# Softmax cross-entropy gradient: the stores of odd rows issued on GpSimd's queue

## The chip, the cores and the metric

The kernel runs on one NeuronCore of a Trainium2 chip. A core has TensorE (PE), VectorE (DVE), ScalarE (ACT), GpSimd (POOL) and SyncE (SP), which run their own instruction queues and meet only at semaphores. Transfers between HBM (the device's main memory) and SBUF (the core's working memory, 128 partitions) are done by 16 DMA engines; an instruction on an engine's queue issues a transfer, and a semaphore tells when it has landed. The metric is the device time of one execution in microseconds (us), the median of several runs; lower is better.

## The reference

For 8 x 1024 = 8192 rows of 8192 logits (fp32, 268 MB) and a label for each row, the kernel computes the gradient of the cross-entropy loss with respect to the logits: softmax of the row, less 1 at the label's column.

```python
logits_max = np.max(logits, axis=-1, keepdims=True)
exp_logits = np.exp(logits - logits_max)
softmax = exp_logits / np.sum(exp_logits, axis=-1, keepdims=True)
...
one_hot[batch_idx, seq_idx, labels] = 1.0
return (softmax - one_hot).astype(np.float32)
```

Every logit is read once and every result, as large as the input, is written once.

## The kernel before

The 8192 rows are cut into B = 32 blocks. A block has G = 2 rows for each of the 128 partitions: partition p of block b holds the two neighbouring rows `(b p j)` with j = 0 and 1. In this text "row t" (t = 0 to 63) means the 128 rows, one for each partition, with b = t // 2 and j = t % 2: a tile of 128 x 8192 fp32, 4.19 MB, with 32 KB contiguous in a partition. Rows with j = 0 are called even, those with j = 1 odd.

The tile X in SBUF has SLOTS = 3 slots of one block each; block b lies in slot b % 3, and all work on it is done in place: the load writes it, the engines turn it into the result, and the store reads it.

Work on row t:

- DVE: the negated maximum along the row into m (`row_max`, TENSOR_REDUCE).
- ACT: exp(x - max) in place, with the sum into s (first ACTIVATE and its ACTIVATION_READ_ACCUMULATOR).
- DVE: r = 1 / s (RECIPROCAL).
- ACT: x * r in place (second ACTIVATE, out<-in X<-X,r).
- DVE: subtract 1 where the column number equals the label (SCALAR_TENSOR_TENSOR with the column numbers `iota`, which stand in PSUM as 16-bit integers). Its entry in `finished[t]` is what the store of the row waits for.

The last row does the last two steps in two halves of 4096 columns.

The order on each queue is written out by hand by the loop over t. DVE's is: reciprocal of t, maximum of t + 1, subtraction of t. ACT's is: exp of t, store of t - 1, scaling of t. So the maximum of the next row stands ahead of the subtraction of this one, and the store of a row stands in ACT's queue ahead of the scaling of the next.

SP issues the loads, all in order and as far ahead as the waits allow. `LOADS` has a letter for each block: "r" is one transfer per row (two a block, each waits for the store of the same row of the block three before), "w" is one transfer for the whole block (8.39 MB, 64 KB contiguous in a partition; it waits for both stores of that earlier block). Blocks 0 to 4 and 26 to 31 are "r", blocks 5 to 25 are "w". Row 1 of block 2 also waits until `iota` is made, as its place is used for that at the start. `STORES` is "r" for all blocks: one store a row, issued by ACT. At the end ACT waits for the stores of the last three blocks.

Every instruction is recorded by the helper `run`, which adds the waits and the semaphore to count up; the last wait rides on the instruction itself, those before it stand in the engine's queue. So nearly all instructions have one line in the profile, L68 (L69 in the changed kernel), and groups are told apart by engine, operation and tile. Each slot has semaphores `got` (loads, one for each of its two pieces) and `put` (stores, the same). POOL makes an identity matrix and the column numbers in the first 8 us and has nothing to do after that. PE does two small transposes of the labels at the start.

Of the kernel before, what the change touches and what calls it, by code (L numbers as in the profile page):

```python
# [8 lines left out]
G = 2  # L9
SLOTS = 3  # L10
# [7 lines left out]
def kernel(  # L18
# [6 lines left out]
    nc = tc.nc  # L25
# [30 lines left out]
    with tc.tile_critical():  # L56
        sem = tc.alloc_semaphore
        got = [[sem(f"got{i}{q}") for q in range(2)] for i in range(SLOTS)]
        put = [[sem(f"put{i}{q}") for q in range(2)] for i in range(SLOTS)]
        lab_got, dve, act, pe, pool = (sem(n) for n in ("lab_got", "dve", "act", "pe", "pool"))  # L60
        count = {}

        def run(engine, waits, counter, method, **operands):

            waits = list(dict.fromkeys(waits))
            for w in waits[:-1]:
                engine.wait_ge(*w)
            instruction = getattr(engine, method)(**operands)  # L68
            for w in waits[-1:]:  # L69
                instruction._wait_ge(*w)  # L70
            step = 16 if method == "dma_start" else 1
            instruction.then_inc(counter, step)
            count[counter.name] = count.get(counter.name, 0) + step
            return counter, count[counter.name]
# [42 lines left out]
        loaded, stored, finished = {}, {}, []  # L117
# [14 lines left out]
        def store(t):  # L132
            b, j = divmod(t, G)
            stored.setdefault(b, [])
            for q, piece in enumerate(PIECES[STORES[b]]):
                ps, js = piece
                if js.stop != j + 1:
                    continue
                w = run(
                    nc.scalar, [finished[t]], put[b % SLOTS][q], "dma_start",  # L140
                    out=o_b[b, ps, js, :], in_=X[ps, b % SLOTS, js, :],
                )
                stored[b].append((piece, w))
# [16 lines left out]
        for t in range(T):  # L160
# [11 lines left out]
            if t > 0:  # L172
                store(t - 1)
# [10 lines left out]
            for c, w in zip(cols, scaled):  # L184
# [4 lines left out]
                )  # L189
            finished.append(w)  # L190
        store(T - 1)
        for b in range(B - SLOTS, B):
            for _, w in stored[b]:
# [31 lines left out]
```

## Time and profile before

| | |
|---|---|
| median of 3 timed runs | 1247.98 us (1247.91 to 1248.11) |
| span of the profiled execution | 1245.7 us; the profile gives no other time for it |
| DVE busy | 1119.2 us (90%), 196 instructions |
| ACT busy | 919.1 us (74%), 194 instructions |
| POOL busy | 7.4 us (1%), 7 instructions |
| bytes moved | 536.98 MB, mean 431 GB/s over the span |
| maximum of a row (DVE) | 64 x 8675 ns |
| subtraction at the label (DVE) | 65 instructions, a full row 8742 ns |
| exp of a row (ACT) | 64 x 7123 ns |
| scaling of a row (ACT) | 65 instructions, a full row 7122 ns |
| issue of a store on ACT's queue | 64 x 338 ns |
| store, issue to landing | 14.3 us at least, 30.8 median, 52.4 at most |
| load, issue to landing | 12.2 us at least; median 26.6 of one row or 33.4 of a block |

A span runs from the first to the last instruction of the profiled execution. Engines DVE, ACT and POOL are busy while they compute; a DMA issue isn't counted as busy. The 40 digits of a "DMA" line are the busy share of the 16 DMA engines in 40 equal slices of the span, in tenths (9 is 90% or more). The rows "q1", "q10" are DMA queues: packets, megabytes and the time that their packets took as a share of the 16 engines' span; q1 belongs to SP's loads and q10 to ACT's transfers. A packet is one contiguous stretch that a DMA engine moves for one queue, 32 or 64 KB here, or the 4 bytes that count up a semaphore. The chain that ended last is followed back from the last instruction, at each step to what released it.

### The profile page before, as it was taken

How to read it: one execution, taken by the hardware profiler on the slowest of the kernel's cores; microseconds unless marked ns; L12 is line 12 of the kernel's file. 1: busy time of each engine (PE TensorE's matmuls, PEld its weight loads, DVE VectorE, ACT ScalarE, POOL GpSimd, SP SyncE). 2: the span in 40 equal slices, each digit the busy share in tenths (PEclk: the TensorE clock that was granted, in tenths of full speed). 3: DMA queues.
4: the chain of work that ended last, by engine and by line, in shares of the span. 5: the costliest groups of instructions: out<-in, count | busy, mean ns of one | idle time of the engine just before them, and what ended most of it. 6: DMA issues, size and time to landing. Idle time of an engine off the chain costs nothing.

```text
span 1245.7 us, 592 instructions
## 1 busy us (share of the span) xinstructions
PE 0.4 (0%) x2; PEld 0.3 (0%) x2; DVE 1119.2 (90%) x196; ACT 919.1 (74%) x194; POOL 7.4 (1%) x7
## 2 busy tenths in 40 slices
PE   0000000000000000000000000000000000000000
PEld 0000000000000000000000000000000000000000
DVE  5999998888988889888998888988889999999893
ACT  3888886778776787767877778777777788887772
POOL 2000000000000000000000000000000000000000
DMA  9999999999999999999999999999999999999998
GB/s 406 417 429 433 438 433 442 437 426 427 430 435 445 439 417 442 426 430 437 432 443 438 420 435 432 430 437 450 420 426 437 436 428 432 437 435 429 432 437 386
DMA packets 15460, 536.98 MB, mean 431 GB/s; under 512 B 1728, under 2 KB 1728, under 8 KB 1760
## 3 DMA queue, kind: packets, MB, share of 16 engines
q1 hardware_dynamic: 6192, 268.44, 50.0%
q10 hardware_dynamic: 9264, 268.51, 49.9%
q14 instruction: 4, 0.03, 0.0%
HBM read 268.50 MB, written 268.44 MB: 431 GB/s over the span
## 4 chain that ended last, share of the span: by engine, by line
DMA 59%; DVE 37%; another core or an unknown queue 2%; ACT 1%; DVEq 0%; issue 0%; PE 0%; SPq 0%; ACTq 0%
DMA X<-in_logits_dram 31%; DMA out_dram<-X 27%; DVE m L68 18%; DVE X L68 18%; ACT X L68 1%; DVE iota L68 0%; DVEq L56 0%; DMA lab_raw<-in_labels_dram 0%; DVE lab_f L68 0%; DVE r L68 0%; PE iota L68 0%; SPq L68 0%; ACTq L68 0%; DVE lab L68 0%
## 5 line engine op out<-in xcount | busy, mean ns | idle before, releaser
L68 DVE TENSOR_REDUCE m<-X 128x1 f32<-128x8192 f32 x64 | 555.2, 8675 | 94.3 <-DMA X<-in_logits_dram 94.3
L68 ACT ACTIVATE X<-X,m 128x8192 f32<-128x8192 f32 x64 | 455.9, 7123 | 188.4 <-DVE m L68 188.4
L68 DVE SCALAR_TENSOR_TENSOR X<-iota,lab,X 128x8192 f32<-128x8192 int16 (+1 forms) x65 | 559.7, 8612 | 4.1 <-ACT X L68 4.1
L68 ACT ACTIVATE X<-X,r 128x8192 f32<-128x8192 f32 (+1 forms) x65 | 456.0, 7017 | 115.9 <-DVE r L68 115.9
L68 DVE RECIPROCAL r<-s 128x1 f32<-128x1 f32 x64 | 9.9, 154 | 7.3 <-ACT X L68 7.3
L68 ACT ACTIVATION_READ_ACCUMULATOR X<-X,m 128x1 f32 x64 | 12.0, 187 | 0.0
L68 DVE CAST lab_f<-lab_raw 32x256 f32<-32x256 int32 x1 | 3.7, 3685 | 4.7 <-DMA lab_raw<-in_labels_dram 4.7
L68 POOL IOTA X<- 128x8192 int16 x1 | 6.9, 6944 | 0.0
L68 DVE TENSOR_SCALAR iota<-X 128x4096 int32<-128x4096 int32 x1 | 4.4, 4427 | 0.1
L68 ACT ACT_TABLE_LOAD x1 | 1.3, 1283 | 1.3 <-SPq L56 1.3
L68 DVE COPY lab<-iota 128x64 f32<-128x64 f32 x1 | 0.2, 225 | 0.5 <-PE iota L68 0.5
L68 PE MATMUL iota<-ident,lab_f 32*128 32x32 f32 x2 | 0.4, 300 | 8.5 <-DVE lab_f L68 8.5
L68 PEld LDWEIGHTS iota<-ident,lab_f 32*128 32x128 f32 x2 | 0.3, 196 | 8.4 <-DVE lab_f L68 8.4
L68 POOL TENSOR_SCALAR_AFFINE_SELECT ident<-ident 32x32 f32<-32x32 f32 x1 | 0.2, 204 | 0.1
L68 POOL MEMSET ident<- 32x32 f32 x1 | 0.1, 115 | 0.5 <-SPq L56 0.5
L209 POOL MEMSET const-bfloat16-1.0<- 128x1 bf16 x1 | 0.1, 107 | 0.0
L209 POOL MEMSET const-uint8-127<- 128x1 uint8 x1 | 0.1, 107 | 0.0
L209 POOL MEMSET const-float32-0.0<- 128x1 f32 x1 | 0.1, 104 | 0.2 <-issue 0.2
L209 POOL MEMSET const-float32-1.0<- 128x1 f32 x1 | 0.1, 104 | 0.0
## 6 DMA issues: line engine op xcount, KB each, us to landing
out_dram<-X ACTq DMA_DIRECT2D x64, 4096.0 KB, 30.8
X<-in_logits_dram SPq DMA_DIRECT2D x22, 4096.0 KB, 26.6
X<-in_logits_dram SPq DMA_DIRECT2D x21, 33.4
lab_raw<-in_labels_dram ACTq DMA_DIRECT2D x1, 64.0 KB, 3.8
```

Of the source, the lines that this page charges most:

```text
L68: instruction = getattr(engine, method)(**operands)
L209: nc = _bacc.Bacc("TRN2", target_bir_lowering=False, num_devices=1)
```

## The change

The store of an odd row (j = 1) is issued by POOL on POOL's own DMA queue, with a semaphore of its own for each slot (`put_pool`). The store of an even row is issued by ACT as before. Both wait for the same subtraction on DVE (`finished[t]`). The loads, their order and what frees them are unchanged: a load waits for the same stores, whose counters for odd rows are now `put_pool`. The final waits on ACT cover both kinds.

```diff
         got = [[sem(f"got{i}{q}") for q in range(2)] for i in range(SLOTS)]
+        put_pool = [sem(f"put_pool{i}") for i in range(SLOTS)]
         put = [[sem(f"put{i}{q}") for q in range(2)] for i in range(SLOTS)]
...
                 if js.stop != j + 1:
                     continue
+                odd = j == G - 1
                 w = run(
-                    nc.scalar, [finished[t]], put[b % SLOTS][q], "dma_start",
+                    nc.gpsimd if odd else nc.scalar, [finished[t]],
+                    put_pool[b % SLOTS] if odd else put[b % SLOTS][q], "dma_start",
                     out=o_b[b, ps, js, :], in_=X[ps, b % SLOTS, js, :],
                 )
```

In the built program ACT's queue loses 32 transfers, POOL's gets 32, one after the other behind its start-up work, each with a wait for DVE. The instructions of DVE, PE and SP stand in the same order as before.

## The prediction

> **What bounds the kernel now.** I read the slices of the page and its DMA queues first, then the queues' shares in single stretches, then the chain that ended last, then ACT's timeline at the end. The page's DMA line and queue rows:
>
> ```profile
> DMA  9999999999999999999999999999999999999998
> ...
> q1 hardware_dynamic: 6192, 268.44, 50.0%
> q10 hardware_dynamic: 9264, 268.51, 49.9%
> ```
>
> q1 carries the loads (SP), q10 the stores (ACT). Together their packets fill 99.9% of the 16 DMA engines' span: the transfers are the bound, and DVE (90%) waits for them. In the trace's packet records every 32 KB packet took 1213 ns, load or store alike, and each engine moves 8 per row of 4.19 MB, so one row's transfer costs 8 x 1.213 = 9.70 us. 64 loads and 64 stores are 128 x 9.70 = 1242 us of a 1245.7 us span. Nothing in a choice of queue can go below that, and only 3.7 us lies outside it.
>
> How the queues share, from the DMA answers for 1180 to 1198 us (loads of one row, "r") and 240 to 266 us (loads of two rows, "w"):
>
> ```profile
> q1 hardware_dynamic: 128, 4.16, 53.5%
> q10 hardware_dynamic: 128, 3.67, 47.2%
> ```
>
> ```profile
> q1 hardware_dynamic: 126, 8.26, 73.5%
> q10 hardware_dynamic: 122, 3.47, 30.9%
> ```
>
> Equal numbers of packets, whatever their size (a "w" load's are 64 KB, a store's 32 KB): the engines take the queues in turn, one packet each. While both have work, one row is loaded per row stored, 19.4 us for the pair.
>
> The end of the chain that ended last, columns start, duration, what:
>
> ```profile
> 1105.48 48.30 DMA out_dram<-X
> 1153.78 0.02 issue
> 1153.79 0.33 SPq L68
> 1154.12 19.00 another core or an unknown queue
> 1173.11 0.02 issue
> 1173.13 26.61 DMA X<-in_logits_dram
> 1199.74 0.02 issue
> 1199.76 8.69 DVE m L68
> 1208.45 8.66 DVE X L68
> ```
>
> The last load lands at 1199.74. A store here takes 48.30 us from issue to landing, against 9.70 us of own transfer: it stands behind earlier stores in ACT's single queue. ACT's timeline shows how that queue is filled:
>
> ```profile
> 1178.46 0.34 ACTq L68 DMA_DIRECT2D out_dram<-X  x1
> ...
> 1197.80 0.34 ACTq L68 DMA_DIRECT2D out_dram<-X  x1
> ...
> 1217.14 0.34 ACTq L68 DMA_DIRECT2D out_dram<-X  x1
> ...
> 1230.18 0.34 ACTq L68 DMA_DIRECT2D out_dram<-X  x1
> ```
>
> These are the stores of rows 60, 61, 62, 63. Row 63's is issued 30.44 us after the last load lands (maximum, exponential, scaling, subtraction, all serial). It lands 14.3 us later (the shortest landing that the tile's answer gives for out_dram), at 1244.49, and the span ends 1.2 us after that. So from 1199.74 to 1244.49 the DMA engines still had 44.75 / 9.70 = 4.6 rows of stores to move. The serial end needs 30.44 + 12.2 (the shortest landing of a row's load, alone on the engines) = 42.6 us. Backlog and serial end match to 2 us: the end costs nothing now only because 1.6 rows of old stores are still queued.
>
> **The change part by part.** ACT loses 32 store issues, 32 x 0.34 = 10.9 us of its queue. ACT already waits 188 us for the maxima and 116 us for r; the issue delays the scaling, which ends a microsecond before DVE is free for it. Worth 0.
>
> POOL gains 32 waits on DVE, each with one DMA. Nothing else stands in POOL's queue after its iota (done by 8.2 us), so nobody is held behind them. SP's loads wait for odd rows on put_pool instead of put: same number of waits, other releaser.
>
> How long POOL takes from the semaphore to the first packet, no row shows. Ends: 0.2 us, as its AFFINE_SELECT (204 ns), and 6.9 us, as its IOTA over 128 partitions. A DMA of 128 rows is nearer in work to the short one, and ACT's own issue is 0.34 us; I take 1.0 us more than ACT and keep 0 to 6.5. In the middle it is covered by the packets of the other queues: a slot has 3 x 38.8 = 116 us to go round and needs 19.4 (load) + 52 (two rows' work) + 9.7 (last store) + about 5 (two issue-and-landing lags of 12.2 - 9.7 = 2.5) = 86 us, so 30 us is spare. At the end it counts once, for row 63, which is odd.
>
> The rate of POOL's packets: nearest row, ACT's 32 KB packet at 1213 ns, so 0. The other end: the label load's 2 KB packets took 98 ns where the rate gives 76; 22 ns more on each of POOL's 32 x 8 packets is 5.6 us. A gain is excluded, for the rate is the same in both directions and on both queues.
>
> The large part is the turns. With stores on two queues, a load gets one turn in three while both hold work: two rows stored per row loaded, 29.1 us per round. DVE finishes no more rows than were loaded, so waiting stores shrink by one row per round. The "r" loads run from 979 to 1173 us, over six such rounds; the backlog in ACT's queue at their start was about one row (a store took 32 us there). It is gone long before the end, and loads wait instead. From then on one store is in flight beside one load, 19.4 us for the pair, the pace that DVE keeps at the end now (its maxima start 19.35 us apart).
>
> How much store work is left when the last load lands: row 63 and row 62 whole, and row 61 nearly whole (now issued 1.9 us before that landing, at 1197.80). Row 60 was issued 21.3 us before, time for 2.2 rows, half of it the load's: 0 to 0.2 of it is left. R = 3.1 rows (3.0 to 3.3), against 4.6 now.
>
> The sum, against the profiled execution's own time. The engines never idle before that landing, so it comes 3.1 rows before the 1244.5 at which all transfers would be through: 1244.5 - 3.1 x 9.70 = 1214.4. Then 30.44 to the last issue, 12.2 for its transfer alone, 1.0 for POOL, 1.2 to the end: 1259.2 us span. The timed runs lie 2.25 us above the span (1247.98 - 1245.73; the profile states no time of its own execution beyond the span): **1261.5 us, 1.1% slower**. With R 3.0 to 3.3 and POOL at 0 to 6.5 the time is 1258.5 to 1268; with 5.6 us of slower packets up to 1273.5.
>
> A rule weighed against that: the page "DMA: Bandwidth & Descriptors" of the Trainium skill, § Issuing engines are not separate DMA queues, says that DMAs from any issuing engine run on the same 16 engines and interleave, so that several issuers save sequencer time alone. The packet turns above agree that they interleave; read as "no effect", the rule gives 1248, which is the first rival's time.
>
> **The rivals.**
>
> *Shares stay as they are* (not slower). If both store queues together got one turn against one for the loads, or POOL's queue were served only in ACT's pauses, backlog would again be 4.5 rows when the last load lands. It decides at R = 4.5: below that each row missing costs 9.7 us. Time 1246 to 1250. For it: only two queues are seen sharing here. Against it: they share strictly by packet, and q1 and q10 belong to different issuers as the third will. A true gain could only come from the 3.7 us outside the transfers, of which 2.2 (first packet) and 1.2 (after the last landing) remain.
>
> *POOL's store is cut into smaller packets.* Turns go by packet, so with 4 KB packets an odd store would need 64 turns per engine, 8 times a load's; it would land only when the other queues are empty. Each load waits for an odd store, so every block would show a bubble of one issue-and-landing lag, 2.5 us. Over 21 to 29 blocks that is 53 to 73 us, and the end stays exposed: 1314 to 1334. For it: POOL's queue is another kind than the two seen. Against it: the instruction names the same 128 rows of 32 KB. The page "DMA: Bandwidth & Descriptors" of the Trainium skill, § SWDGE vs HWDGE vs iDMA, says that a packet is preferably at most 4096 B; by that the time would be this rival's. Here the two queues seen send 32 and 64 KB whole, and no trace shows POOL's.
>
> *POOL's transfers pay more per packet.* A tenth more on 32 rows is 32 x 0.97 = 31 us, on top of the exposed end: 1292, or 1267 to 1293 with the 5.6 us as the lower end. For it only the 22 ns of the short packets.
>
> **How the numbers follow.** Forecast (end exposed, whole packets at full rate) 0.62; dearer packets 0.14; small packets 0.10; shares unchanged 0.10; a gain by something unseen 0.04. A difference of up to 0.2%, 2.5 us, counts as no change here, about what a measurement can tell. Slower 0.62 + 0.14 + 0.10 = 0.86, same 0.10, faster 0.04. The range holds the first, the unchanged one and most of the dearer packets, 1247 to 1290; small packets and a gain are left out. The likeliest case's own range is 1258.5 to 1268.
>
> **What the changed profile would show.** A third queue with 32 x 144 = 4608 packets (256 data packets and 32 counters on each of 16 engines) and 25% share; many more means small packets, a larger share dearer ones. Landing of stores falls below 30 us near the end, and loads there wait 50 us instead. The last load lands near 1214; the DMA line falls below 9 in its last slice or two, with some 14 us idle after that landing and none before. DVE and ACT durations stay. The prediction is wrong if the last load lands near 1200 still, or if the DMA engines idle before 1200.

## The result and the profile after

The changed kernel takes 1299.52 us (median of 4 runs, 1298.33 to 1300.72) against 1247.97 us before: a ratio of 1.0414 with a 95% interval of 1.0399 to 1.0428. It is 51.6 us slower. The sign was forecast; the size, +13.5 us, was not, and the time lies 9.5 us above the upper end of the range. The profiled execution took 1299.05 us, with a span of 1297.3 us, 51.6 us longer than the span before. Ratios here and below leave out an execution over 1.5% longer than the fastest of its kernel, while medians take in all, so that a ratio can lie under the quotient of the medians.

The page of the changed kernel: its DMA line, queue rows (packets, MB, share of 16 engines), POOL's new group (busy, mean ns, idle before), and the transfers (KB each, median us from issue to landing).

```profile
DMA  9999999999999999999999999999999999999966
...
q1 hardware_dynamic: 6192, 268.44, 49.3%
q0 software_dynamic: 4608, 134.22, 24.5%
q10 hardware_dynamic: 4656, 134.29, 24.2%
...
L69 POOL DMA_DIRECT2D out_dram<-X x32 | 17.1, 536 | 1258.7 <-DVE r L69 1228.1
...
out_dram<-X ACTq DMA_DIRECT2D x32, 4096.0 KB, 20.4
out_dram<-X POOLq DMA_DIRECT2D x32, 4096.0 KB, 30.0
X<-in_logits_dram SPq DMA_DIRECT2D x22, 4096.0 KB, 48.1
```

There is a third queue with exactly the 4608 packets forecast: 4096 whole ones of 32 KB and 512 counters. The three shares add up to 98.0%. That splits the loss. Packet time is 0.980 x 1297.3 = 1271.4 us, against 0.999 x 1245.7 = 1244.5 before: the same packets took 26.9 us more per engine. The other 24.7 us are idle time: 2.0% of 1297.3 = 25.9 us against 1.2. (The shares are rounded to 0.1%, about 1 us.)

Where each lies is seen in the windows. Columns: window, its length, busy us of PE, PEld, DVE, ACT and POOL (instructions), PEclk, DMA share, GB/s. Before first, then the changed kernel. The cut at 1199.7 (before) and at 1253.0 (after) is the landing of the last load.

```profile
150.00:300.00 150.00, 0.00 (x0) 0.00 (x0) 134.15 (x25) 110.65 (x23) 0.00 (x0) 1.00 1.00 433
300.00:950.00 650.00, 0.00 (x0) 0.00 (x0) 581.94 (x102) 480.24 (x102) 0.00 (x0) 1.00 1.00 434
950.00:1199.70 249.70, 0.00 (x0) 0.00 (x0) 239.41 (x42) 199.24 (x43) 0.00 (x0) 1.00 1.00 432
1199.70:1245.70 46.00, 0.00 (x0) 0.00 (x0) 26.29 (x5) 20.13 (x5) 0.00 (x0) 1.00 0.93 402
```

```profile
150.00:300.00 150.00, 0.00 (x0) 0.00 (x0) 121.31 (x22) 100.36 (x21) 1.59 (x3) 1.00 0.97 403
300.00:950.00 650.00, 0.00 (x0) 0.00 (x0) 573.88 (x101) 474.88 (x100) 9.03 (x17) 1.00 1.00 427
950.00:1200.00 250.00, 0.00 (x0) 0.00 (x0) 218.72 (x38) 178.87 (x38) 3.19 (x6) 1.00 1.00 417
1200.00:1253.00 53.00, 0.00 (x0) 0.00 (x0) 42.07 (x9) 35.14 (x9) 1.06 (x2) 1.00 0.85 359
1253.00:1297.30 44.30, 0.00 (x0) 0.00 (x0) 26.23 (x5) 20.88 (x5) 0.53 (x1) 1.00 0.66 284
```

- The last row is the exposed end that was forecast: 44.3 us with the engines at 0.66, that is 0.34 x 44.3 = 15.1 us idle ("some 14 us idle after that landing" was forecast).
- Between 300 and 950 us the engines are as busy as before (1.00) and move less (427 GB/s instead of 434). The same holds from 950 to 1200 us (417 instead of 432). Busy engines at a lower rate mean longer packets.
- From 150 to 300 us and from 1200 to 1253 us they also idle, before the last load.

The waits of DVE, before and then after (total us, times, longest), show who pays. The total grows by 52.7 us, about the loss itself; DVE's and ACT's durations are unchanged.

```profile
DVE m L68 <- DMA X<-in_logits_dram: 94.3, 25, 6.9
```

```profile
DVE m L69 <- DMA X<-in_logits_dram: 147.0, 29, 24.4
```

The timeline of DVE at the end of the changed kernel (start, duration, instruction, idle before and its releaser):

```profile
1234.79 8.69 DVE L69 TENSOR_REDUCE m<-X 128x1 f32<-128x8192 f32 x1 [2.19 <-DMA X<-in_logits_dram]
...
1252.94 8.69 DVE L69 TENSOR_REDUCE m<-X 128x1 f32<-128x8192 f32 x1 [0.74 <-DMA X<-in_logits_dram]
```

Row 63's maximum starts at 1252.94, behind a load that landed at 1252.92; before it was 1199.76. From there nothing is late: POOL's last store is issued at 1283.61 and the span ends 44.4 us after the landing.

### What the packet records add

The sizes 32 and 64 KB have usual durations of 1213 and 2418 ns in both kernels. In what follows the **stretch** of a kernel is the time that its packets took beyond these (611 ns for 16 KB), per engine; a **gap** is a time in which no engine moves a store packet, between the first store and the last load's landing; and **rows left** is the store work still to move when the last load lands, in rows of 9.70 us, as in the prediction.

| kernel | median us | last load lands | its landing over the 16 engines | rows left | stretch | of that 300 to 950 us |
|---|---|---|---|---|---|---|
| before | 1247.97 | 1199.7 | 1.3 us | 4.4 | 2.3 us | 0.5 us |
| changed | 1299.52 | 1252.9 | 20.5 us | 3.0 | 29.3 us | 10.1 us |

Of the 29.3 us, 19.3 lie on the load packets, 6.6 on POOL's and 3.4 on ACT's. The landing of the last load is spread over 20.5 us: the first engine is through with it at 1232.4, the last at 1252.9. The engines no longer move in step. This does not build up evenly: the loads that land from 325 to 991 us are spread over 3.4 to 3.6 us, those from 1041 us on over 10.3 to 20.5 us. 10.6 us of the stretch lie between 950 us and the last landing, against 0.0 in before.

The last load of a whole block (block 25) lands at 991.2 us against 966.9 before. So 24.3 of the 53.2 us by which the last load comes later arise up to there, and 28.9 behind it.

Behind its first 5 us the trace of before holds one place with a stretch of over 1 us per engine. It was not looked at for the prediction. Its windows around the first store, issued at 47 us while loads run alone (columns as above):

```profile
40.00:48.00 8.00, 0.00 (x0) 0.00 (x0) 8.00 (x3) 6.15 (x3) 0.00 (x0) 1.00 1.06 459
48.00:52.00 4.00, 0.00 (x0) 0.00 (x0) 4.00 (x1) 4.00 (x1) 0.00 (x0) 1.00 0.90 262
52.00:60.00 8.00, 0.00 (x0) 0.00 (x0) 8.00 (x2) 6.88 (x2) 0.00 (x0) 1.00 1.03 446
```

For 4 us the rate falls to 262 GB/s (a packet counts where it starts, so a short window is coarse: the three together give 414). The last two load packets on an engine ahead of its first store packet, 32 KB each and begun at about 48.9 and 50.8 us, take 0.66 and 0.50 us more than usual on average. Later on, before has no gap of over 4.2 us, and its two of 4.2 us cost 0.00. The changed kernel has 20 gaps of 6.8 to 17.7 us (median 8.7), with loads alone on the engines, and 19 of them end with a store of POOL. Counting the load packets that start from 3.5 us before the next store packet to 6 us behind it, these 20 starts hold 11.2 us of stretch, 0.36 to 1.29 each. Only two of them, 0.7 us, lie behind 950 us.

### The profile page after: what moved, and what is told of

Read it like the earlier page. It is cut to its first block, busy times and chain, and to the rows that moved or that the text cites. A ratio compares the mean times of both kernels' runs of the same rounds, so it can differ in the third digit from the quotient of the medians.

```text
span 1297.3 us, 592 instructions
## 1 busy us (share of the span) xinstructions
PE 0.4 (0%) x2; PEld 0.3 (0%) x2; DVE 1117.0 (86%) x196; ACT 919.0 (71%) x194; POOL 24.6 (2%) x39
## 3 DMA queue, kind: packets, MB, share of 16 engines
q0 software_dynamic: 4608, 134.22, 24.5%
## 4 chain that ended last, share of the span: by engine, by line
DMA 55%; DVE 39%; issue 3%; another core or an unknown queue 2%; ACT 1%; POOLq 0%; POOL 0%; PE 0%; ACTq 0%; DVEq 0%; SPq 0%
DMA X<-in_logits_dram 28%; DMA out_dram<-X 26%; DVE m L69 19%; DVE X L69 19%; ACT X L69 1%; DMA lab_raw<-in_labels_dram 0%; DVE iota L69 0%; DVE r L69 0%; DVE lab_f L69 0%; POOLq L56 0%; POOL out_dram L69 0%; PE iota L69 0%; DVE lab L69 0%; ACTq L223 0%
## 5 line engine op out<-in xcount | busy, mean ns | idle before, releaser
L69 POOL DMA_DIRECT2D out_dram<-X x32 | 17.1, 536 | 1258.7 <-DVE r L69 1228.1
L69 DVE CAST lab_f<-lab_raw 32x256 f32<-32x256 int32 x1 | 1.1, 1079 | 7.3 <-DMA lab_raw<-in_labels_dram 7.3
## 6 DMA issues: line engine op xcount, KB each, us to landing
X<-in_logits_dram SPq DMA_DIRECT2D x22, 4096.0 KB, 48.1
```

## The experiments

Theories that the runs had to tell apart: **turns** (the prediction's: three queues take packets in turn, the backlog of stores is gone at the end); **POOL's kind** (its software queue makes transfers dearer); **third queue** (three queues at once upset the engines); **dry starts** (a store side that runs empty and starts again beside loads alone costs time, whoever issues it).

### All stores on POOL

Against the kernel before:

```diff
-                    nc.scalar, [finished[t]], put[b % SLOTS][q], "dma_start",
+                    nc.gpsimd, [finished[t]], put[b % SLOTS][q], "dma_start",
```

> All 64 stores on POOL's queue, none on ACT's: two queues share again, as before, but one is POOL's. Turns (two store queues starve the loads, and the end is exposed): no exposed end, the last load lands some 45 us before the last store, as before. Start toll (each transfer issued by POOL stretches the packets under way by 0.54 to 0.84 us on every engine, the stretched packets of the changed kernel divided by its 32 transfers): 64 x 0.54 to 0.84 = 35 to 54 us, 1283 to 1302. Third queue (packets stretch because three queues run and the engines fall out of step): 1248, no stretched packets.

1251.61 us (1250.45 to 1253.32), ratio 1.0030 [1.0019, 1.0041]. Its page:

```profile
DMA  9999999999999999999999999999999999999998
...
q1 hardware_dynamic: 6192, 268.44, 49.9%
q0 software_dynamic: 9216, 268.44, 49.7%
```

Twice as many transfers on POOL's queue as in the changed kernel, and a fourteenth of its loss (1251.61 - 1247.85 before on the same chip = 3.8 us). Two queues, shares equal, 4.39 rows left, last load at 1201.5, stretch 3.5 us. With stores always queued, POOL's kind is not what costs, and a fixed toll per store issued by POOL falls too. The issue instruction (536 ns instead of ACT's 338) is hidden as well: were it on the path 64 times, 64 x 0.2 = 12.7 us would be seen.

### Tiny stores on POOL, the rest on ACT

Against the kernel before: ACT stores all of the even rows and all but the last 128 columns of the odd ones; POOL stores those.

```diff
+                odd = j == G - 1
+                cut = V - 128 if odd else V
...
-                    out=o_b[b, ps, js, :], in_=X[ps, b % SLOTS, js, :],
+                    out=o_b[b, ps, js, :cut], in_=X[ps, b % SLOTS, js, :cut],
                 )
+                if odd:
+                    w = run(
+                        nc.gpsimd, [finished[t]], put_pool[b % SLOTS], "dma_start",
+                        out=o_b[b, ps, js, cut:], in_=X[ps, b % SLOTS, js, cut:],
+                    )
...
```

> ACT stores all rows, but of odd rows only 8064 columns; POOL stores the last 128 columns of odd rows (64 KB, 512 B a partition). As many transfers on POOL as in the changed kernel, a sixty-fourth of the bytes; its turns are negligible. Start toll: 32 x 0.54 to 0.84 = 17 to 27 us, 1265 to 1275. Toll by bytes on POOL's queue: under 1 us, 1248 to 1249. Third queue out of step: as by bytes, 1248 to 1250.

1248.42 us, ratio 1.0008 [0.9998, 1.0017]. Its third queue:

```profile
q0 software_dynamic: 1024, 2.10, 0.4%
```

32 waits and issues on POOL and a third queue with next to no work in it cost nothing that can be measured. What costs in the changed kernel is where the bytes go.

### The exposed end without POOL

The kernel before, with the loads of blocks 26 to 31 in two column halves, so that a load's packets are 16 KB against a store's 32: loads get a third of the bytes, as with three queues.

```diff
-                w = run(
-                    nc.sync, free, got[b % SLOTS][q], "dma_start",
-                    out=X[ps, b % SLOTS, js, :], in_=x_b[b, ps, js, :],
-                )
+                n = 2 if b >= 26 else 1
+                for i in range(n):
+                    c = slice(i * V // n, (i + 1) * V // n)
+                    w = run(
+                        nc.sync, free, got[b % SLOTS][q], "dma_start",
+                        out=X[ps, b % SLOTS, js, c], in_=x_b[b, ps, js, c],
+                    )
```

> The kernel before, with the loads of blocks 26 to 31 issued in two halves of 4096 columns, so that their packets are 16 KB against 32 KB of the stores: loads get a third of the bytes while stores are queued, as in the changed kernel, without POOL. Turns: store backlog drains, the last load lands 14 to 16 us later (1214 to 1216), DMA engines idle 13 to 14 us at the end, time 1260 to 1263. If the late last load of the changed kernel comes from POOL's queue and not from shares: 1248. Start toll and third queue: no stretched packets here.

1268.06 us, ratio 1.0162 [1.0147, 1.0177]. Its windows, cut at the landing of its last load:

```profile
950.00:1222.50 272.50, 0.00 (x0) 0.00 (x0) 239.76 (x42) 199.24 (x43) 0.00 (x0) 1.00 1.00 421
1222.50:1265.30 42.80, 0.00 (x0) 0.00 (x0) 26.29 (x5) 19.71 (x5) 0.00 (x0) 1.00 0.63 272
```

2.77 rows left, and an end of 42.8 us with the engines at 0.63. No POOL and no third queue: the share of turns alone makes the exposed end. The last load lands 6.5 us later than expected at most (1216), and the time is 5 us above the upper expectation; the stretch of 7.3 us against 2.3, which was not expected here, is as large.

### POOL in one part of the run alone

Against the changed kernel: POOL stores odd rows in blocks 26 to 31 alone, or in blocks 0 to 25 alone; ACT the others.

```diff
-                odd = j == G - 1
+                odd = j == G - 1 and b >= 26     # the end alone
...
+                odd = j == G - 1 and b < 26      # the middle alone
```

> POOL stores the odd rows of blocks 26 to 31 alone (6 stores); all others on ACT. Turns: end exposed, plus 14 us, 1262. Start toll: 6 x 0.54 to 0.84 = 3 to 5 us more, 1265 to 1267. Third queue: engines out of step in this phase as in the changed kernel, whose packets were stretched by 9.5 us per engine after 950 us and whose engines idled some 9 us more than forecast: 1275 to 1281.

> POOL stores the odd rows of blocks 0 to 25, ACT all rows of blocks 26 to 31: the complement of POOL at the end alone. Turns: the backlog is gone when the last phase begins and one queue builds it up again by 2 us a row over 12 rows, so the end stays exposed by about 10 us, 1258. On top of that the packets stretched before 950 us in the changed kernel (16 us per engine) and its idle stretch at 200 to 250 us (4 us): 1278. If the stretched packets come only when POOL serves the last phase too: 1258.

The end alone: 1263.92 us, ratio 1.0127 [1.0111, 1.0143], +16.1 us. Its windows, cut at the landing of its last load:

```profile
300.00:950.00 650.00, 0.00 (x0) 0.00 (x0) 581.95 (x102) 480.19 (x102) 0.00 (x0) 1.00 1.00 434
950.00:1218.70 268.70, 0.00 (x0) 0.00 (x0) 238.85 (x42) 198.82 (x43) 2.79 (x5) 1.00 0.99 426
1218.70:1262.00 43.30, 0.00 (x0) 0.00 (x0) 26.29 (x5) 19.65 (x5) 0.53 (x1) 1.00 0.65 281
```

This is the prediction's mechanism by itself: the middle as before (434 GB/s), the last load at 1218.7 with 2.9 rows left, an end of 43.3 us. It takes 1263.92 where the sum gave 1261.5, and the third-queue theory's 1275 to 1281 falls.

The middle alone: 1286.71 us, ratio 1.0321 [1.0303, 1.0339], +38.9 us, with the last load at 1238.4, a stretch of 23.6 us and 3.08 rows left. That is 8.7 us above the upper expectation. It has an exposed end too, from a deficit that it carries over, and the two parts don't add up exactly (16.1 + 38.9 = 55.0 against 51.6). Block 25's load lands at 993.8 us here and at 967.8 us with POOL at the end alone (966.9 before): some 27 us arise in the blocks up to 25, where the prediction had counted nothing. Behind 950 us the stretch is 4.3 us with POOL in the middle alone and 2.3 us with POOL at the end alone, against 10.6 us in the changed kernel, which has both.

### Even rows on POOL instead of odd

Against the changed kernel:

```diff
-                odd = j == G - 1
+                odd = j == 0
```

> POOL stores the even rows, ACT the odd ones. In blocks 5 to 25 of the changed kernel the odd store is the one that starts while loads run alone, and the load packets under way were stretched 4 to 9 us after it. If that is POOL's kind of queue meeting loads that run alone: here ACT's store meets them, no stretched packets in these blocks, 1258 to 1268. If it is any store that starts beside loads alone, or three queues as such: as the changed kernel, 20 to 30 us of stretched packets per engine, 1290 to 1300.

1291.93 us (1278.40 to 1298.23), ratio 1.0317 [1.0251, 1.0382]. Its profile is of its longest execution. Now 18 of 19 gaps of over 4.5 us end with a store of ACT, and the loss stays (stretch 28.6 us, 20 to 30 expected); "POOL's store meets a lone load" isn't the cause.

### Hardware queues alone, with other packet sizes

The kernel before, the block loads issued as two row transfers (32 KB packets, the same waits); and the kernel before with one store per block in blocks 5 to 25 (64 KB packets). No store is issued by POOL in either.

```diff
-                w = run(
-                    nc.sync, free, got[b % SLOTS][q], "dma_start",
-                    out=X[ps, b % SLOTS, js, :], in_=x_b[b, ps, js, :],
-                )
+                for one in [slice(j, j + 1) for j in range(js.start, js.stop)]:
+                    w = run(
+                        nc.sync, free, got[b % SLOTS][q], "dma_start",
+                        out=X[ps, b % SLOTS, one, :], in_=x_b[b, ps, one, :],
+                    )
```

> The kernel before (all stores on ACT), each load of a whole block issued as two transfers of one row, so packets of 32 KB against 32 KB: stores get half the bytes, drain sooner, and loads run alone for some 5 us before the odd store starts, with two hardware queues only. By turns alone: about 1252 (the store backlog at the start of the last phase is smaller). If any store that starts beside loads alone stretches their packets: 21 x 0.45 = 9 us more, 1261, with stretched load packets 4 to 9 us after odd stores. If POOL's queue is needed: none, 1252.

```diff
-STORES = "rrrrrrrrrrrrrrrrrrrrrrrrrrrrrrrr"
+STORES = "rrrrrwwwwwwwwwwwwwwwwwwwwwrrrrrr"
```

> The kernel before (all stores on ACT), blocks 5 to 25 stored whole (8.39 MB, 64 KB packets, issued when the odd row is done), so that loads run alone for long stretches before each store. The store of the even row waits for the odd one, so the time itself may rise by some tens of us from idle engines. Any store beside loads alone: 21 starts x 0.45 = 9 us of stretched load packets per engine. POOL's queue needed: under 1 us in these blocks.

Two row transfers: 1272.44 us, ratio 1.0201 [1.0177, 1.0224]. Block stores: 1346.18 us, ratio 1.0788 [1.0766, 1.0809]. The windows of the first and of the second:

```profile
300.00:950.00 650.00, 0.00 (x0) 0.00 (x0) 567.38 (x99) 471.37 (x100) 0.00 (x0) 1.00 1.00 424
```

```profile
300.00:950.00 650.00, 0.00 (x0) 0.00 (x0) 525.60 (x93) 433.29 (x93) 0.00 (x0) 1.00 0.95 395
```

The first has the changed kernel's sign (1.00 busy, 424 GB/s), the second also idles, 43.7 us before its last load lands, as the store of an even row waits for the odd one. Both expectations were too low: 1272.44 against 1261 at most, and a stretch of 45.2 us against 9 (16.3 in the first). So neither POOL nor a third queue is needed: what the lossy middles share is a store side that runs empty and starts again. The 21 gaps of over 4.5 us with block stores last 10.5 us in the median, 20.1 at most, and their ends hold 1.1 us of stretch each; the 17 of the first variant last 6.7 us in the median and hold 0.4 us each.

### Smaller store packets, meant as a repair

The changed kernel with each store in two column halves (16 KB packets), so that the two store queues together would get one row for each row loaded; in all blocks, and in blocks 0 to 25 alone.

```diff
-                w = run(
-                    nc.gpsimd if odd else nc.scalar, [finished[t]],
+                n = 2                            # or: 2 if b < 26 else 1
+                for i in range(n):
+                    c = slice(i * V // n, (i + 1) * V // n)
+                    w = run(
+                        nc.gpsimd if odd else nc.scalar, [finished[t]],
...
-                    out=o_b[b, ps, js, :], in_=X[ps, b % SLOTS, js, :],
+                        out=o_b[b, ps, js, c], in_=X[ps, b % SLOTS, js, c],
```

> The changed kernel (odd rows on POOL, even rows on ACT, three queues, the same bytes on each), with every store issued in two halves of 4096 columns, so that store packets are 16 KB. Two store queues then take 2 x 16 KB a round against 32 or 64 KB of the loads: the shares of the kernel before. Shares (all of the loss comes from loads losing turns: exposed end, and stores that run dry and start again beside loads alone): last load back at 1200 to 1207, stretched packets under 5 us per engine. A 16 KB packet took 611 ns where half of 1213 is 606.5, 64 x 16 x 4.5 ns = 4.6 us: 1252 to 1257. Three queues or POOL's kind as such: as the changed kernel, 1290 or more.

> The same halves for blocks 0 to 25 alone; blocks 26 to 31 stored as in the changed kernel. Shares: the loss of the middle is gone and that of the end stays, as in the kernel with POOL at the end alone (1264) plus 3.8 us for 52 rows of 16 KB packets: 1264 to 1270. Three queues or POOL's kind as such: 1290 or more.

Both missed: 1295.08 us (1283.89 to 1306.35), ratio 1.0349 [1.0297, 1.0402], and 1322.83 us, ratio 1.0615 [1.0594, 1.0637]. The profile of the first is of its longest execution, 1306.35 us. Its windows, and then one of the changed kernel:

```profile
300.00:950.00 650.00, 0.00 (x0) 0.00 (x0) 546.65 (x95) 451.31 (x95) 15.80 (x30) 1.00 0.98 408
1000.00:1200.00 200.00, 0.00 (x0) 0.00 (x0) 187.69 (x34) 155.81 (x34) 5.28 (x10) 1.00 1.00 430
```

```profile
1000.00:1200.00 200.00, 0.00 (x0) 0.00 (x0) 175.17 (x31) 144.77 (x31) 2.66 (x5) 1.00 1.00 415
```

The last phase did what was meant: 430 GB/s, 3.89 rows left, a landing spread of 1.8 us, and all of this with three queues at work. The middle got worse: 408 GB/s, 21.8 us of stretch; with halves in the middle alone, whose profile is not of its longest execution, the same window shows 413 GB/s and 18.8 us. In these 650 us of the first, both store queues move packets for 228 us, POOL's alone for 259 and ACT's alone for 53, and one store queue of 16 KB packets gets a fifth of the bytes against 64 KB loads. The expectation took for granted that both were always filled. With halves in the first 26 blocks alone the bad middle is followed by the exposed end. Its loss of 75.0 us is more than that of the half stores and of POOL at the end together (47.2 + 16.1 = 63.3), and what adds the rest is not shown. No version was found that beats the kernel before.

### A start by itself

To price one start: 32 block loads in sequence, and a store of one row behind every second of them, issued by ACT or by POOL. All computation is left out.

```diff
...
+            loaded[b] = run(
+                nc.sync, free, got[i][0], "dma_start", out=X[:, i, :, :], in_=x_b[b, :, :, :]
+            )
+            if b % 2 == 1:
+                stored[b] = run(
+                    nc.scalar, [loaded[b]], put[i][0], "dma_start",      # or nc.gpsimd
+                    out=o_b[b, :, 0, :], in_=X[:, i, 0, :],
+                )
...
```

> A measure of the start alone: no computation (the output is not the gradient: 16 row tiles of logits are copied, the rest is not written). SP loads all 32 blocks one behind the other into the three slots, ACT stores the even row of every second block when it has landed, so 16 stores each start on an empty store queue beside loads that run alone. In the kernel before, the first store (at 47 us) did that, and the load packets under way took 0.6 and 0.5 us longer on every engine: if each such start costs 1.1 us, 18 us of stretched packets per engine in sum. If a start costs nothing and the loss of the middle comes from something else in the loop: under 2 us. Transfers alone are 32 x 19.35 + 16 x 9.7 = 774 us, so a span of 778 or 795.

> The same with the 16 stores on POOL's queue (the same parts of the computation left out). If a start costs by itself, whatever the queue: the same 18 us within 3 us. If POOL's kind of queue makes it dearer: above 25 us. If it is free: under 2 us.

789.24 us with ACT and 788.51 us with POOL. The windows of the one and the other (POOL busy, PEclk, DMA share, GB/s):

```profile
100.00:700.00 600.00, 0.00 (x0) 1.00 1.00 432
```

```profile
100.00:700.00 600.00, 6.37 (x12) 1.00 1.00 433
```

Spans 787.6 and 787.5 us, between the expected 778 and 795; the 15 starts beside loads hold 3.3 and 3.5 us of stretch. ACT and POOL are equal once more in the sum. The price of a start is 0.5 us at ACT's first and 1.0 at POOL's, 0.05 at the last ones, 0.2 on average, though every gap between stores lasts 21 to 24 us. A dry start beside lone loads is thus not always worth half a microsecond; its length of dryness doesn't set the price, and what does stays open.

All kernels that compute, by gaps of over 4.5 us and stretch:

| kernel | gaps | stretch us |
|---|---|---|
| before | 0 | 2.3 |
| tiny stores on POOL | 0 | 2.4 |
| all stores on POOL | 0 | 3.5 |
| POOL at the end alone | 1 | 5.1 |
| small loads at the end | 7 | 7.3 |
| block loads as two transfers | 17 | 16.3 |
| POOL in the middle alone | 18 | 23.6 |
| half stores in the middle alone | 21 | 27.2 |
| even rows on POOL | 19 | 28.6 |
| changed | 20 | 29.3 |
| half stores | 20 | 32.3 |
| block stores | 21 | 45.2 |

A kernel without gaps has next to no stretch, with two queues or with three, with POOL or without. The two go together; the table doesn't show how the one makes the other.

## Why the prediction was right in sign and wrong in size

**Right.** The transfers bound the kernel before and after. The queues take turns by packet: 3.0 rows of stores were left at the last load against the forecast 3.1, and from that landing to the end it took 44.4 us against 44.8. The page "DMA: Bandwidth & Descriptors" of the Trainium skill, § Queues, rings and completion order, says that each engine goes round its queues packet by packet; the trace agrees for a software queue too: from 989 to 999 us of the changed kernel, with work on all three, they start 41 (POOL), 49 (loads) and 40 (ACT) packets. The exposed end alone measured +16.1 us (POOL at the end) and +20.2 us (small loads), against a forecast of +13.5. POOL's lag was small, under the 1.0 us taken: row 63's store begins 0.30 us behind the subtraction and lands 11.35 us later, against 0.03 and 11.1 us for ACT with small loads at the end. ACT's lost issues were worth nothing; all 64 of them could go without a gain.

**Rivals.** Small packets fell: 4608 packets, all data in 32 KB. Shares unchanged fell: loads landed 48.1 us after issue and the backlog went. Dearer POOL packets came nearest in time (1267 to 1293) by the wrong mechanism: of 29.3 us of stretch POOL's own packets hold 6.6, close to the bound of 5.6, while the loads hold 19.3; and all stores on POOL cost 3.8 us.

**Wrong.** The step that failed is "The engines never idle before that landing, so it comes 3.1 rows before the 1244.5", together with a packet duration held fixed for the queues that were there already. The last load landed 38.5 us after the forecast 1214.4. Of that, stretched packets are 29.3 - 2.3 = 27.0 us, and idle engines ahead of the landing 10.8 us (25.9 in all less the 15.1 at the end); together 37.8, which closes to 1 us. The error is wholly ahead of the last load. By the landing of block 25's load 24.3 us of it have arisen, where the forecast had nothing; the other 14 us come in the last phase, on top of the delay that was forecast there.

In its place the runs showed this. With two queues a block's stores are moved faster than a single queue would move them: the turn that the loads lose empties the store side early. The loads then run alone, the next store starts on an empty side, and load packets under way take longer. In the last phase the engines also fall out of step (a load's landing spread over 10 to 20.5 us), and a transfer is through only with its slowest engine. The prediction had worked out the lost turns and drew from them only the end ("It is gone long before the end, and loads wait instead"), not what a store side that empties does in between. Shown by runs: it isn't POOL's kind (all on POOL, even rows on POOL, starts by themselves), nor three queues as such (tiny stores, last phase of the half stores), and two hardware queues alone reach +24.6 and +98 us when shares or late stores empty the store side. Argued from packet records, not isolated: that the restarts themselves cause the stretch. The probe gave 0.2 us per start on average, the kernels with computation 0.4 to 1.1. For the last phase of the changed kernel, with 10.6 us of stretch and 0.7 at dry starts, no cause is shown.

Its own condition had named the place: it said the prediction is wrong "if the DMA engines idle before 1200", and between 150 and 300 us the DMA share is 0.97. And the packets at 48 us of before were there to be read: the one place in that trace where a store started beside loads alone. "Every 32 KB packet took 1213 ns" holds for the median; 32 load packets there took 0.2 to 1.1 us more. Two smaller slips changed nothing: the first load of one row is issued at 956 us, not 979, and by packets 4.4 rows were left before, not 4.6.

The same page of the Trainium skill, § Issuing engines are not separate DMA queues, says that issuing on several engines saves only sequencer time. Read as "no effect", that nearly fits one queue in place of another, +0.3%; the split measured 4.1% slower, as a further queue takes a further turn.

Open: what sets the price of a start (means of 0.2 to 1.1 us); why the engines fall out of step in the last phase (a landing spread of 20.5 us in the changed kernel, 28.7 with half stores in the middle, 1.8 with half stores throughout); and the changed kernel's stretch outside the 20 starts counted, 29.3 - 11.2 = 18.1 us.

## What to carry to other kernels

In a loop that is bound by its transfers, the queue of waiting stores is what covers the serial end and keeps loads and stores mixed, so count turns per packet before a stream is split over queues: here each queue with work got one packet, and the split stream took its second turn from the loads. Then ask for every stage, not for the end alone, whether a side will run empty, and look in the trace of before for the place where a stream starts beside another one: the packets there that take longer than usual are the nearest price (1.2 us here). Full busy digits don't exclude a loss; compare GB/s by stage too.

## What the runs showed of the hardware that was not expected

- When a store started on an empty store side, load packets just ahead of and beside its first packets took longer: 1.2 us in two 32 KB packets per engine at 48 us of the kernel before, and with 64 KB loads anything from 0.05 us (late starts of the probe) to 1.1 us (block stores).
- POOL's software queue moved whole 32 KB packets with a median of 1213 ns, as ACT's hardware queue does; all 64 stores on it cost 0.3%.
- The 16 engines can drift apart: the last load's landing is spread over 1.3 us before, over 20.5 us in the changed kernel, and over 20.6 us with block stores on hardware queues alone. In both of the latter the spread stays under 4 us from 325 to 991 us and grows behind 1000 us.
- Kernels with such a middle vary from run to run: 1278 to 1298 us with even rows on POOL, 1284 to 1306 us with half stores, where the kernel before stays within 0.1% of its median.
